# Layer-norm boundaries whose GpSimd work goes to VectorE, and eight more weight tiles split early and kept in DRAM

## The chip, the cores and the metric

The kernel runs on one core of one Trainium2 chip. The metric is device microseconds (us) of one execution. TensorE is called PE, VectorE DVE, ScalarE ACT, GpSimd POOL, and SyncE, which issues nearly every transfer, SP.

## The reference, cut to what matters

Two layers over 512 frames of width 1024. Layer 0 mixes with gated linear attention (GLA), layer 1 with chunked softmax attention (16 heads); each is followed by a squared-ReLU MLP of width 4096. Four times, after each mixer and each MLP, comes a layer norm:

```python
u = x * (1.0 + sc1) + sh1
y = gla_mixer(u, ...) if layer == 0 else chunk_attention(u, ...)
x = layer_norm(ALPHA * x + (1.0 + g1) * y, ln_g[i, 0], ln_b[i, 0])
u = x * (1.0 + sc2) + sh2
y = squared_relu_mlp(u, ff_w1[i], ff_w2[i])
x = layer_norm(ALPHA * x + (1.0 + g2) * y, ln_g[i, 1], ln_b[i, 1])
```

Shift, scale and gate come from a conditioning vector through `w_ada`. Everything is float32, and the result has to keep close to float32 precision.

## The kernel before, in words

**Layout.** Features lie on the 128 partitions, so x is eight tiles `xs[0..7]` of 128x512 (features x frames). A layer norm is a sum over partitions and over the eight tiles.

**Split weights.** Each weight is cut into 512 KB tiles of 128x1024. A tile is loaded (`raw`), cast to a short format on ACT (`whi`), and the rest is formed on DVE (`wlo = raw - whi`). Each product is three matmuls (`mm3`: hi·hi, hi·lo, lo·hi). The order of this work is the list `plan`; `fill(n)` walks it until n tiles are ready. Kinds of unit: `w` and `p` load and split into the four `wp` slots (`p` with the subtraction on POOL), `f` and `F` into tiles of the `act` pool (first products of the next MLP), `a` is a unit of `w_ada`, `c` loads and splits a tile and writes both halves to DRAM, and `x`, `X` read such halves back. There are five `raw` slots. In before, 18 tiles are kept in this way: 14 of `a_qk` (attention's q and k projections) and four of `a_o` (its output projection).

**Order.** Instructions on DVE, ACT, POOL and PE are issued in the order in which the program calls them (`InOrder`); each engine executes its own list in order. SP's list is put in order by the scheduler.

**A boundary.** `boundary()` finishes the output products of a mixer or MLP, adds them to x, and normalises. Tiles 0 to 3 are finished first (`part`, `ev`), then tiles 4 to 7 in two halves of 256 frames (`half_mm`, `half_ev`). To keep the variance exact, a common shift is subtracted from x first (`shift_mm`). Two accumulators hold the sum (`accz`) and the sum of squares (`accq`); in the names of the trace both are `af`, as are the squares. `stats1(hf)` sums them over partitions with `ones_c` on PE, forms the variance (`ve`) and 1/sqrt; `stats2` refines it (`y`). Then every tile is centred (minus the mean `ps`, or its copy `mn`), scaled by `y`, and turned into the next u (`ar`: hi on ACT, lo on DVE). The first four products of the next MLP (`fg`) take u half by half, 96 matmuls of 256 columns for each half. In before, POOL does a part of the subtractions of the shift, most of the sums of squares, the centring and scaling of the odd tiles and five small products (`ln_cols`).

Four boundaries are run: B1 after GLA (about 200 to 261 us), B2 after MLP 0 (about 560 to 608), B3 after attention (about 805 to 876; with `late` order), B4 after MLP 1 (the last 20 us; its output is the result). B2 has no `fg`: its u goes to the value passes of attention (`vfill`: `v_mm(0,fw,0)`, `v_mm(1,vw,0)`, `v_mm(0,fw,1)`, `v_mm(1,vw,1)`), which use `a_v` kept in `act` tiles (`fhi`, `flo`) and `wp` tiles. Behind the value passes come the products of q and k, first with `a_qk[0]`, then `a_qk[8]`. Their weights are, in before, the next two `w` units of the plan; the 14 others are read back from DRAM.

Of the kernel before, what the change touches and what calls it, by code (L numbers as in the profile page):

```python
# [59 lines left out]
def trunk(ctx, tc, xT, c, ada, cols, gk1, gk2, w_qk, w_v, w_g, w_go, a_qk, a_v, a_tab,  # L60
# [128 lines left out]
    def emit_unit():  # L189
# [26 lines left out]
        lo_of(G if kind in "pF" else V, lo, raw, hi)  # L216
# [70 lines left out]
    add_units([a_v[k] for k in range(4, 8)])  # L287
    add_units([a_qk[0], a_qk[8]])
# [18 lines left out]
    def ln_cols(l, i, nxt):  # L307
# [4 lines left out]
        if nxt is not None:  # L312
# [5 lines left out]
            tt(G, a1, g, mS, ALU.mult)  # L318
            tt(G, b1, b, mS, ALU.mult)
            tt(G, b1, b1, mH, ALU.add)  # L320
            ag = const.tile([P, 8], F32, name=nm("ag"))
            ab = const.tile([P, 8], F32, name=nm("ab"))
            G.tensor_scalar(out=ag, in0=g, scalar1=ALPHA, scalar2=None, op0=ALU.mult)
            G.tensor_scalar(out=ab, in0=b, scalar1=ALPHA, scalar2=None, op0=ALU.mult)
# [5 lines left out]
    def boundary(src, l, gt, open_lnt, mk_cols, fg_evac, events=None, final=False, vfill=None):  # L330
# [25 lines left out]
        def ev(m):  # L356
            stt(xs[m], pss[m], mod(l, gt, m), xs[m], ALU.mult, ALU.add)
            if m == 1:
                tt(V, accz, xs[0], xs[1], ALU.add)

        def shift_mm():
            pm = bank()
            T.matmul(pm, ones_h, accz, start=True, stop=True)
            A.copy(out=shift, in_=pm)
            for j in (4, 5, 6, 7):
                if j > 5 or "shift" in events:
                    tt(G, xs[j], xs[j], shift, ALU.subtract)
                else:
                    tt(V, xs[j], xs[j], shift, ALU.subtract)
            for j in (0, 1):  # L370
                tt(V, xs[j], xs[j], shift, ALU.subtract)

        events = events or [(0, range(8)), (1, range(8)), (2, range(8)), "shift", (3, range(8))]
        late = "shift" not in events
        for e in events:
            if e == "shift":
                shift_mm()
                continue
# [5 lines left out]
            if left[m] == 0:  # L384
                ev(m)
                if m < 3 and "shift" in events:
                    fill(3)
        lnc = mk_cols()
# [3 lines left out]
        def start_acc():  # L392
            for m in (2, 3):
                tt(V, xs[m], xs[m], shift, ALU.subtract)
            tt(V, accz, xs[0], xs[1], ALU.add)
            A.activation(out=accq, in_=xs[0], func=AF.Square)
            tt(G if "shift" in events else V, accq, accq, sq_of(xs[1], S), ALU.add)
            for m in (2, 3):
                tt(V, accz, accz, xs[m], ALU.add)
                if late and m == 3:  # L400
                    q = shift
                    A.activation(out=q, in_=xs[m], func=AF.Square)
                else:
                    q = sq_of(xs[m], S)
                tt(G, accq, accq, q, ALU.add)

        if "shift" in events:
            start_acc()
        else:
            fill_f(4)  # L410
# [6 lines left out]
        def half_ev(m, hf, ps, j, mid=lambda: None):  # L417
            hs = slice(hf * HT, (hf + 1) * HT)
            xh = xs[m][:, hs]
            stt(xh, ps[:, j * HT:(j + 1) * HT], mod(l, gt, m), xh, ALU.mult, ALU.add)  # L420
# [5 lines left out]
            tt(V if m == 7 or (final and hf) else G, accq[:, hs], accq[:, hs], q, ALU.add)  # L426
# [6 lines left out]
        def stats1(hf, last=None, fill_in=None):  # L433
# [24 lines left out]
            for k in (2, 4):  # L458
                tt(V, xs[k][:, hs], xs[k][:, hs], dm, ALU.subtract)
            st[hf] = dm, ve, y0  # L460

        def stats2(hf):
            hs = slice(hf * HT, (hf + 1) * HT)
# [3 lines left out]
            tt(V, xs[6][:, hs], xs[6][:, hs], dm, ALU.subtract)  # L467
# [3 lines left out]
            st[hf] = y  # L471
            for k in (1, 3, 7) if final and hf else (1, 3, 5, 7):
                tt(G, xs[k][:, hs], xs[k][:, hs], y, ALU.mult)
# [4 lines left out]
        def ap1(hf, p):  # L478
            ks = (2 * p, 2 * p + 1)
            hs = slice(hf * HT, (hf + 1) * HT)  # L480
            k = ks[0]
            tt(V, xs[k][:, hs], xs[k][:, hs], st[hf], ALU.mult)
            for k in ks:
                xh = xs[k][:, hs]
                a1, b1 = lnc["a"][:, k:k + 1], lnc["b1"][:, k:k + 1]
                us[k] = tl("u", 4)
                A.activation(out=un[k][:, 0, hs], in_=xh, func=AF.Identity, scale=a1, bias=b1)
                if k % 2:
                    V.tensor_scalar(out=us[k], in0=xh, scalar1=a1, scalar2=b1, op0=ALU.mult, op1=ALU.add)
                else:  # L490
                    A.activation(out=us[k], in_=xh, func=AF.Identity, scale=a1, bias=b1)

        def ap2(hf, p):
            hs = slice(hf * HT, (hf + 1) * HT)
            for k in (2 * p, 2 * p + 1):
                lo_of(V, un[k][:, 1, hs], us[k], un[k][:, 0, hs])

        def norm(hf, k):
            hs = slice(hf * HT, (hf + 1) * HT)
            tt(V, xs[k][:, hs], xs[k][:, hs], st[hf], ALU.mult)  # L500
# [20 lines left out]
        for m in range(4, 8):  # L521
            pa[m] = bank()
            half_mm(m, 0, pa[m], 0)
            if m == 4 and "shift" not in events:
                shift_mm()
                start_acc()
            half_ev(m, 0, pa[m], 0)
        pb = {m: bank() for m in range(4, 8)}
        half_mm(4, 1, pb[4], 0)
        if late:  # L530
            half_mm(5, 1, pb[5], 0, range(3))
            half_ev(4, 1, pb[4], 0)
            stats1(0)
            half_mm(5, 1, pb[5], 0, range(3, KT))
            stats2(0)
        else:
            stats1(0)
            stats2(0)
            half_ev(4, 1, pb[4], 0, (lambda: norm(0, 0)) if final else lambda: None)
            half_mm(5, 1, pb[5], 0)  # L540
        if final:
            affine(0, 1, (1, 3))
            affine(0, 0, (0, 2))
            half_ev(5, 1, pb[5], 0, lambda: norm(0, 2))
            half_mm(6, 1, pb[6], 0)
            affine(0, 3, (1, 3))
            affine(0, 2, (0, 2))
            half_ev(6, 1, pb[6], 0)
            half_mm(7, 1, pb[7], 0)
            affine(0, 5, (5, 7))  # L550

# [4 lines left out]
            stats1(1, lambda: half_ev(7, 1, pb[7], 0), fill_in)  # L556
            affine(0, 7, (5, 7))
            affine(0, 4, (4, 6))
            affine(0, 6, (4, 6))
            stats2(1)  # L560
            norm(1, 0)
            affine(1, 0, (0,))
            norm(1, 2)
            affine(1, 2, (2,))
            affine(1, 1, (1,), True)
            norm(1, 4)
            affine(1, 4, (4, 5))
            norm(1, 5)
            affine(1, 5, (4, 5))
            norm(1, 6)  # L570
            affine(1, 3, (3, 6), True)
            affine(1, 6, (3, 6), True)
            affine(1, 7, (7,))
            return None
        ap1(0, 0)
        half_ev(5, 1, pb[5], 0)
        ap1(0, 1)
        ap2(0, 0)
        half_mm(6, 1, pb[6], 0)
        half_ev(6, 1, pb[6], 0)  # L580
        ap1(0, 2)
        ap2(0, 1)
        half_mm(7, 1, pb[7], 0)
        half_ev(7, 1, pb[7], 0)
# [9 lines left out]
        n = 3 if late else 2  # L594
# [703 lines left out]
```

## Time and profile before

| what | value |
|---|---|
| median of 3 runs | 1222.27 us (1222.24 to 1222.6) |
| the profiled execution | 1222.72 us |
| its span, first to last instruction | 1220.9 us |
| mean granted TensorE clock | 0.990 |
| busy: PE, DVE, ACT, POOL | 1181.6, 831.1, 544.8, 176.6 us |
| HBM read, written | 174.37 MB, 20.97 MB |

Busy time of PE comes close to the span, and so the idle stretches of PE, and those at half clock, are what can be won or lost. All times within the program are counted from the start of the span.

### The profile page before, as it was taken

The page shows a single profiled execution, that of the slowest core. Times are in us where ns is not written, and L with a number is a line of the kernel's source. Part 1 is how long each engine was busy: PE and PEld are TensorE (multiplying, and loading weights), DVE is VectorE, ACT ScalarE, POOL GpSimd, SP SyncE. Part 2 cuts the span into 40 slices and gives each one's busy share as a digit, 9 for nine tenths or more (in the row PEclk, how much of TensorE's full clock was granted, in tenths as well). Part 3 has the DMA queues.
Part 4 walks back from the last instruction along what each step waited for, and adds up shares of the span by engine and source line. Part 5 has one row for each costly group of instructions (what it writes and reads, how often), then busy time and mean ns, then how long its engine had stood idle before and what let it go on. Part 6 is the DMA issues. An engine that isn't in the chain of part 4 may idle for free.

```text
span 1220.9 us, 15202 instructions
## 1 busy us (share of the span) xinstructions
PE 1181.6 (97%) x5742; PEld 985.9 (81%) x5742; DVE 831.1 (68%) x1260; ACT 544.8 (45%) x853; POOL 176.6 (14%) x189
## 2 busy tenths in 40 slices
PE   9999999899999999999899999998999999999995
PEld 5888888788888888888788786678888888888885
DVE  6788589777676677658834878898764443443467
ACT  4564545474243342342536656654641422322324
POOL 1000003610000000005511222235200000000035
PEclk9999999999999999999999999999899999999998
DMA  9756435028889889844026431321155232332201
GB/s 350 257 187 218 170 104 188 3 76 306 291 302 344 295 301 336 297 157 156 31 74 224 155 118 63 130 85 55 62 196 152 90 104 86 102 105 88 94 10 69
DMA packets 58282, 196.33 MB, mean 161 GB/s; under 512 B 6561, under 2 KB 10913, under 8 KB 58210
## 3 DMA queue, kind: packets, MB, share of 16 engines
q1 hardware_dynamic: 58210, 195.37, 46.1%
q8 instruction: 45, 0.74, 0.2%
q14 instruction: 27, 0.22, 0.1%
HBM read 174.37 MB, written 20.97 MB: 160 GB/s over the span
## 4 chain that ended last, share of the span: by engine, by line
PE 77%; DVE 13%; ACT 4%; POOL 3%; issue 2%; ACTq 0%; DVEq 0%; POOLq 0%
PE ps L47 76%; DVE af L47 5%; DVE x L47 3%; ACT af L47 2%; DVE ar L47 2%; POOL af L47 1%; DVE u L47 1%; POOL x L47 1%; DVE wlo L47 1%; PE warm L47 1%; ACT ar L47 1%; DVE d L47 1%; DVE y L47 1%; DVE t L47 0%; DVE raw L47 0%
## 5 line engine op out<-in xcount | busy, mean ns | idle before, releaser
L47 PE MATMUL ps<-ar,whi 128*128 128x512 f32 (+1 forms) x2880 | 822.1, 373 | 0.2 <-DVE ar L47 0.2
L47 PEld LDWEIGHTS ps<-ar,whi 128*128 128x128 f32 x2880 | 526.7, 190 | 96.4 <-issue 2.4
L47 PE MATMUL ps<-ar,wlo 128*128 128x512 f32 (+1 forms) x1440 | 526.0, 372 | 0.2 <-DVE wlo L47 0.2
L47 PEld LDWEIGHTS ps<-ar,wlo 128*128 128x128 f32 x1440 | 273.3, 190 | 46.9 <-DVE wlo L47 0.8
L47 ACT CAST whi<-raw 128x1024 fp32r<-128x1024 f32 (+1 forms) x169 | 169.5, 1010 | 204.8 <-PE ps L47 168.6
L47 DVE TENSOR_TENSOR wlo<-raw,whi 128x1024 fp32r<-128x1024 f32 x160 | 200.2, 1256 | 20.9 <-ACT whi L47 19.1
L47 DVE SCALAR_TENSOR_TENSOR x<-ps,mods,x 128x512 f32<-128x512 f32 (+1 forms) x96 | 63.0, 657 | 123.1 <-PE ps L47 123.1
L47 POOL TENSOR_TENSOR x<-x,af 128x512 f32<-128x512 f32 x14 | 25.4, 1843 | 808.7 <-ACT af L47 808.7
L47 DVE TENSOR_TENSOR h<-r 128x512 f32<-128x512 f32 (+1 forms) x72 | 49.2, 688 | 85.5 <-ACT r L47 84.7
L47 ACT ACTIVATE r<-ps 128x512 f32<-128x512 f32 (+1 forms) x72 | 39.1, 549 | 133.0 <-PE ps L47 132.8
L47 DVE SCALAR_TENSOR_TENSOR raw<-raw,csil 128x1024 f32<-128x1024 f32 x80 | 96.8, 1217 | 0.0
L47 PE MATMUL ps<-ar,fhi 128*128 128x256 f32 (+1 forms) x320 | 70.9, 317 | 6.8 <-DVE ar L47 5.9
L47 DVE TENSOR_TENSOR ar<-h,ar 128x512 fp32r<-128x512 f32 (+1 forms) x72 | 45.6, 633 | 39.5 <-ACT ar L47 38.4
L47 ACT CAST ar<-h 128x512 fp32r<-128x512 f32 (+1 forms) x72 | 41.2, 572 | 51.0 <-DVE h L47 51.0
L47 PEld LDWEIGHTS ps<-ar,fhi 128*128 128x128 f32 x320 | 53.9, 198 | 10.6 <-DVE ar L47 7.1
L47 PE MATMUL ps<-whi,ar 128*128 128x512 f32 x192 | 60.6, 390 | 0.0
L47 POOL PARTITION_ALL_REDUCE mb<-af x16 | 31.7, 1984 | 131.0 <-DVE af L47 123.9
L47 PE MATMUL ps<-ar,flo 128*128 128x256 f32 (+1 forms) x160 | 49.9, 312 | 0.0
L47 ACT ACTIVATE af<-x 128x256 f32<-128x256 f32 (+1 forms) x48 | 22.7, 486 | 57.6 <-POOL af L47 31.8
L47 PEld LDWEIGHTS ps<-whi,ar 128*128 128x128 f32 x192 | 36.0, 188 | 7.6
L47 ACT CAST fhi<-raw 128x1024 fp32r<-128x1024 f32 x30 | 31.4, 1049 | 23.7 <-DMA raw<-a_qk 12.2
L47 ACT ACTIVATE af<-af 128x1024 f32<-128x1024 f32 (+2 forms) x48 | 32.0, 698 | 20.9 <-DVE af L47 20.4
(149 smaller groups left out, 1139.4 us busy)
## 6 DMA issues: line engine op xcount, KB each, us to landing
raw<-f SPq DMA_DIRECT2D x128, 512.0 KB, 4.3
raw<-ada SPq DMA_DIRECT2D x80, 512.0 KB, 4.6
hraw<-ada SPq DMA_DIRECT2D x16, 512.0 KB, 9.0
raw<-a_qk SPq DMA_DIRECT2D x16, 512.0 KB, 5.4
khi_q<-fhi SPq DMA_DIRECT2D x14, 512.0 KB, 3.6
klo_q<-flo SPq DMA_DIRECT2D x14, 512.0 KB, 4.9
whi<-khi_q SPq DMA_DIRECT2D x14, 512.0 KB, 3.3
wlo<-klo_q SPq DMA_DIRECT2D x14, 512.0 KB, 4.3
```

What stands on the lines that cost most here:

```text
L47: r = f(*a, **k)
```

## The change

Three things are done.

First, in all four boundaries POOL's work goes to DVE: subtraction of the shift, sums of squares, centring, scaling, the five small products, and the subtraction of `p` and `F` units. The copy `mn` of the mean goes; u of the odd tiles goes from DVE to ACT. The order within a boundary is written anew with smaller helpers (`sub`, `cen`, `ap`, `lo`). Second, the shift is taken from tile 0 alone (times 2) in place of the sum of tiles 0 and 1. Third, eight more `c` units (`a_o` 4 to 7 and the first four tiles of MLP 1, `f1[1]` 0 to 3) stand in the plan behind the last `a_v` tiles and ahead of `a_qk[0]` and `a_qk[8]`; at the end of attention these eight tiles are read back (`x`, and the new kind `Y`, which reads into `act` tiles) instead of being loaded and split there.

```diff
@@ emit_unit
-        if kind in "xX":
-            hi, lo = split_w(kind == "X")
+        if kind in "xXY":
+            hi, lo = split_w(kind != "x")
...
-            ready_w.append((hi, lo))
+            (ready_f if kind == "Y" else ready_w).append((hi, lo))
...
-        lo_of(G if kind in "pF" else V, lo, raw, hi)
+        lo_of(V, lo, raw, hi)
@@ add_out
-            plan.append(("X", ("o", i)) if early and i < 4 else ("p" if i < pool else "w", u))
+            plan.append(("X" if i < 4 else "x", ("o", i)) if early else ("w", u))
...
-            plan.extend(("fF"[i // 2], u) for i, u in enumerate(fgs))
+            plan.extend(("Y", ("f", i)) for i in range(4))
@@ the plan
     add_units([a_v[k] for k in range(4, 8)])
+    more = [(("o", i), a_o[i]) for i in range(4, 8)] + [(("f", i), f1[1, i]) for i in range(4)]
+    for m in more:
+        plan.append(("c", m))
     add_units([a_qk[0], a_qk[8]])
@@ boundary
+        def sub(*js):
+            for j in js:
+                tt(V, xs[j], xs[j], shift, ALU.subtract)
 
         def shift_mm():
             pm = bank()
-            T.matmul(pm, ones_h, accz, start=True, stop=True)
-            A.copy(out=shift, in_=pm)
-            for j in (4, 5, 6, 7):
-                if j > 5 or "shift" in events:
-                    tt(G, xs[j], xs[j], shift, ALU.subtract)
...
+            T.matmul(pm, ones_h, xs[0], start=True, stop=True)
+            A.activation(out=shift, in_=pm, func=AF.Copy, scale=2.0)
...
             if e == "shift":
                 shift_mm()
+                if not late:
+                    sub(4, 5, 6, 7, 0, 1, 2)
...
         def start_acc():
-            for m in (2, 3):
-                tt(V, xs[m], xs[m], shift, ALU.subtract)
-            tt(V, accz, xs[0], xs[1], ALU.add)
             A.activation(out=accq, in_=xs[0], func=AF.Square)
-            tt(G if "shift" in events else V, accq, accq, sq_of(xs[1], S), ALU.add)
...
+            q = [shs[:, 1, :], shs[:, 1 if late else 0, :]]
+            for m in (1, 2, 3):
+                A.activation(out=q[m % 2], in_=xs[m], func=AF.Square)
+                tt(V, accz, xs[0] if m == 1 else accz, xs[m], ALU.add)
+                tt(V, accq, accq, q[m % 2], ALU.add)
...
             mid()
-            tt(V if m == 7 or (final and hf) else G, accq[:, hs], accq[:, hs], q, ALU.add)
+            tt(V, accq[:, hs], accq[:, hs], q, ALU.add)
...
-            mn = tl("mn", 1)
-            A.copy(out=mn, in_=dm)
...
-            for k in (1, 3, 5, 7):
-                tt(G, xs[k][:, hs], xs[k][:, hs], mn, ALU.subtract)
...
+            cen(hf, *range(n0))
...
-            for k in (1, 3, 7) if final and hf else (1, 3, 5, 7):
-                tt(G, xs[k][:, hs], xs[k][:, hs], y, ALU.mult)
...
+        half_ev(4, 1, pb[4], lambda: stats1(0, 2))
+        stats2(0)
+        half_mm(5, 1, pb[5], 0)
+        ap(0, 0, 1)
+        lo(0, 0)
+        half_ev(5, 1, pb[5])
+        cen(0, 2, 3)
```

**How it moves instructions: SP, ahead of the first q product.** In before, SP's list goes from the last `a_v` load straight to the two loads of `a_qk`, which are followed by loads for later and by the first read-back of a kept tile (`khi_q`, `klo_q` are the halves in DRAM):

```order
L213 DMA raw_5196<-a_v 128x1024
L213 DMA raw_5385<-a_qk 128x1024
L213 DMA raw_5391<-a_qk 128x1024
L213 DMA raw_6749<-a_o 128x1024
L213 DMA raw_6793<-a_o 128x1024
L213 DMA raw_6799<-a_o 128x1024
L980 DMA tab_c<-a_tab 128x16
L213 DMA raw_6805<-a_o 128x1024
L213 DMA raw_6886<-f 128x1024
L197 DMA whi_5457<-khi_q_2536 128x1024
```

Of the change, the same place. Five loads of `c` units and eight writes stand above these rows; the rows begin with the writes of the fifth unit, and the load of `a_qk[0]` is the last:

```order
L209 DMA khi_f_5421<-fhi_5417 128x1024
L210 DMA klo_f_5422<-flo_5418 128x1024
L204 DMA raw_5425<-f 128x1024
L204 DMA raw_5435<-f 128x1024
L204 DMA raw_5445<-f 128x1024
L209 DMA khi_f_5431<-fhi_5427 128x1024
L210 DMA klo_f_5432<-flo_5428 128x1024
L209 DMA khi_f_5441<-fhi_5437 128x1024
L210 DMA klo_f_5442<-flo_5438 128x1024
L209 DMA khi_f_5451<-fhi_5447 128x1024
L210 DMA klo_f_5452<-flo_5448 128x1024
L213 DMA raw_5455<-a_qk 128x1024
```

The loads of `a_qk` have moved behind eight loads and sixteen writes of the `c` units. On ACT the eight casts, and on DVE the eight subtractions, of these units stand behind the `vt` copies that follow `v_mm(0,fw,1)` and ahead of the cast and subtraction of `a_qk[0]`.

**DVE in B1, from the last half of the first 256 frames on.** Of before; `af_1561` holds both accumulators, `af_1562` the squares, `x_94` to `x_101` are `xs[0..7]`:

```order
L47 TENSOR_TENSOR af_1561<-af_1561,x_101 128x256
L47 TENSOR_TENSOR af_1561<-af_1561,af_1562 128x256
L47 SCALAR_TENSOR_TENSOR ve_1923<-ps_1916,d_1919 128x256
L47 TENSOR_TENSOR x_94<-x_94,ps_1916 128x256
L47 TENSOR_TENSOR x_96<-x_96,ps_1916 128x256
L47 TENSOR_TENSOR x_98<-x_98,ps_1916 128x256
L47 TENSOR_TENSOR d_1936<-y_1932 128x256
L47 TENSOR_TENSOR x_100<-x_100,ps_1916 128x256
L47 SCALAR_TENSOR_TENSOR d_1936<-d_1936,ve_1923 128x256
L47 SCALAR_TENSOR_TENSOR y_1940<-d_1936,y_1932 128x256
L47 SCALAR_TENSOR_TENSOR x_98<-ps_1888,mods,x_98 128x256
L47 TENSOR_TENSOR af_1561<-af_1561,x_98 128x256
```

Of the change:

```order
L47 TENSOR_TENSOR af_1570<-af_1570,x_101 128x256
L47 TENSOR_TENSOR af_1570<-af_1570,af_1571 128x256
L47 SCALAR_TENSOR_TENSOR x_98<-ps_1887,mods,x_98 128x256
L47 TENSOR_TENSOR af_1570<-af_1570,x_98 128x256
L47 SCALAR_TENSOR_TENSOR ve_1923<-ps_1918,d_1921 128x256
L47 TENSOR_TENSOR x_94<-x_94,ps_1918 128x256
L47 TENSOR_TENSOR x_95<-x_95,ps_1918 128x256
L47 TENSOR_TENSOR af_1570<-af_1570,af_1571 128x256
L47 TENSOR_TENSOR d_1932<-y_1927 128x256
L47 SCALAR_TENSOR_TENSOR d_1932<-d_1932,ve_1923 128x256
L47 SCALAR_TENSOR_TENSOR y_1935<-d_1932,y_1927 128x256
L47 TENSOR_TENSOR x_94<-x_94,y_1935 128x256
```

The next tile's addition (`x_98<-ps`) has moved up into the wait for the statistics, only two tiles are centred ahead of `y`, and the odd tile `x_95` is now DVE's. From `ve` to the eighth lo part of u for the first 256 frames DVE has 44 instructions in this new order. POOL's list shrinks from 166 rows to 58, and none of these is left in a boundary.

## Rows read from the trace of the kernel before

**Rows 1.** Waits, whole span: us in total, times, longest us

```profile
PE ps L47 <- DVE af L47: 12.6, 9, 3.8
```

**Rows 2.** Timeline of PE, B1: start, us, what, count [idle before <- releaser]

```profile
223.24 1.22 PE L47 MATMUL ps<-af,ones_c 128*128 128x256 f32 x2 [3.81 <-DVE af L47]
...
249.78 0.39 PE L47 MATMUL ps<-ar,fhi 128*128 128x256 f32 x1 [1.56 <-DVE ar L47]
...
261.27 0.63 PE L47 MATMUL ps<-ar,whi 128*128 128x512 f32 x2
```

**Rows 3.** Timeline of DVE, B1

```profile
201.71 2.40 DVE L47 TENSOR_TENSOR x<-x,af 128x512 f32<-128x512 f32 x2 [0.75 <-ACT af L47]
...
210.75 1.29 DVE L47 TENSOR_TENSOR x<-x,af 128x512 f32<-128x512 f32 x2
...
222.76 0.42 DVE L47 TENSOR_TENSOR af<-af,af 128x256 f32<-128x256 f32 x1 [4.08 <-POOL af L47]
```

**Rows 4.** Timeline of POOL, B1

```profile
201.83 7.92 POOL L47 TENSOR_TENSOR x<-x,af 128x512 f32<-128x512 f32 x4 [195.00 <-ACT af L47]
```

**Rows 5.** Timeline of DVE, B3 and the end of attention

```profile
809.18 3.50 DVE L47 TENSOR_TENSOR wlo<-raw,whi 128x1024 fp32r<-128x1024 f32 x3
...
849.23 0.47 DVE L47 SCALAR_TENSOR_TENSOR x<-ps,mods,x 128x256 f32<-128x256 f32 x1
...
850.66 0.42 DVE L47 TENSOR_TENSOR x<-x,y 128x256 f32<-128x256 f32 x1
851.00 0.40 DVE L47 TENSOR_SCALAR u<-x,a,b 128x256 f32<-128x256 f32 x1
```

**Rows 6.** Timeline of PE, end of attention and B3

```profile
813.40 0.50 PE L47 MATMUL ps<-ar,fhi 128*128 128x512 f32 x1 [1.60 <-DVE ar L47]
...
835.51 0.70 PE L47 MATMUL ps<-af,ones_c 128*128 128x256 f32 x2 [2.99 <-DVE af L47]
836.55 0.70 PE L47 MATMUL ps<-af,ones_c 128*128 128x256 f32 x2 [0.34 <-DVE af L47]
...
861.78 0.58 PE L47 MATMUL ps<-ar,fhi 128*128 128x256 f32 x1 [2.34 <-DVE ar L47]
...
875.96 0.63 PE L47 MATMUL ps<-ar,whi 128*128 128x512 f32 x2
```

**Rows 7.** Stretches of 25 us: PE, PEld, DVE, ACT, POOL busy, PEclk, DMA, GB/s

```profile
625.00:650.00 25.00, 25.00 (x112) 20.72 (x111) 5.36 (x7) 8.08 (x12) 0.00 (x0) 1.00 0.45 168
...
850.00:875.00 25.00, 22.52 (x160) 22.02 (x159) 19.90 (x41) 13.91 (x30) 8.79 (x9) 0.86 0.06 23
```

**Rows 8.** Timeline of PE, last value pass and first q product

```profile
629.87 0.39 PE L47 MATMUL ps<-whi,ar 128*128 128x512 f32 x1
...
640.75 0.62 PE L47 MATMUL ps<-ar,whi 128*128 128x512 f32 x2
```

**Rows 9.** Timeline of ACT, value passes

```profile
629.39 0.59 ACT L47 COPY vt<-ps 128x512 f32<-128x512 f32 x1 [9.83 <-PE ps L47]
632.79 1.05 ACT L47 CAST whi<-raw 128x1024 fp32r<-128x1024 f32 x1 [2.81 <-PE ps L47]
```

**Rows 10.** Transfers, 605 to 607: issues, KB each, us from issue to landing

```profile
raw<-a_qk SPq DMA_DIRECT2D x1, 512.0 KB, 3.4
```

**Rows 11.** Transfers, 10 to 28, where loads alone are issued

```profile
DMA packets 2307, 7.35 MB, mean 409 GB/s; under 512 B 256, under 2 KB 256, under 8 KB 2307
```

**Rows 12.** Transfers, 471 to 474, where writes of kept tiles and loads mix

```profile
klo_o<-flo SPq DMA_DIRECT2D x1, 512.0 KB, 5.5
raw<-a_o SPq DMA_DIRECT2D x1, 512.0 KB, 6.3
```

**Rows 13.** Timeline of all engines, B4

```profile
1208.08 0.63 PE L47 MATMUL ps<-af,ones_c 128*128 128x256 f32 x2
...
1212.46 1.29 DVE L47 TENSOR_TENSOR x<-x,y 128x256 f32<-128x256 f32 x2
1212.57 2.49 POOL L47 TENSOR_TENSOR x<-x,y 128x256 f32<-128x256 f32 x3 [0.42 <-DVE y L47]
```

More of the change, by code (lines that the diff above doesn't have):

```diff
@@ L328, in trunk, with boundary @@
     cur = {}
-    def boundary(src, l, gt, open_lnt, mk_cols, fg_evac, events=None, final=False, vfill=None):
+    def boundary(src, l, gt, open_lnt, mk_cols, fg_evac, events=None, final=False, vfill=None, late=False):
+        lnc = mk_cols()
         acc = act_f()
@@ L385, in boundary @@
                 ev(m)
-                if m < 3 and "shift" in events:
+                if m < 3 and not late:
                     fill(3)
-        lnc = mk_cols()
         lnt = open_lnt()
@@ L392, in start_acc @@
         def start_acc():
-            for m in (2, 3):
-                tt(V, xs[m], xs[m], shift, ALU.subtract)
-            tt(V, accz, xs[0], xs[1], ALU.add)
             A.activation(out=accq, in_=xs[0], func=AF.Square)
-            tt(G if "shift" in events else V, accq, accq, sq_of(xs[1], S), ALU.add)
[L398 to L407, printed above, removed]
+            q = [shs[:, 1, :], shs[:, 1 if late else 0, :]]
[3 more added lines that the diff above has]
+                tt(V, accq, accq, q[m % 2], ALU.add)
+        if late:
+            fill_f(4)
+        else:
+            sub(3)
             start_acc()
-        else:
-            fill_f(4)
         def half_mm(m, hf, ps, j, ks=range(KT)):
@@ L431, in tl, with cen, stats1 @@
             return lnt.tile([P, HT], F32, tag=tag, bufs=bufs, name=nm(tag))
-        def stats1(hf, last=None, fill_in=None):
+        def cen(hf, *ks):
+            hs = slice(hf * HT, (hf + 1) * HT)
+            for k in ks:
+                tt(V, xs[k][:, hs], xs[k][:, hs], st[hf][0], ALU.subtract)
+        def stats1(hf, n0, last=None, fill_in=None):
             hs = slice(hf * HT, (hf + 1) * HT)
@@ L523, in boundary @@
             half_mm(m, 0, pa[m], 0)
[L524 to L527, printed above, removed]
+            if late:
+                if m == 4:
+                    sub(4, 0, 1, 2, 3)
+                    start_acc()
+                else:
+                    sub(m)
+            half_ev(m, 0, pa[m])
         pb = {m: bank() for m in range(4, 8)}
         half_mm(4, 1, pb[4], 0)
[L530 to L534, printed above, removed]
+        if final:
+            stats1(0, 4)
             stats2(0)
[L536 to L539, printed above, removed]
+            half_ev(4, 1, pb[4], lambda: norm(0, 0))
             half_mm(5, 1, pb[5], 0)
-        if final:
+            affine(0, 0, (0, 2))
+            cen(0, 4, 5)
+            norm(0, 1)
             affine(0, 1, (1, 3))
-            affine(0, 0, (0, 2))
-            half_ev(5, 1, pb[5], 0, lambda: norm(0, 2))
+            half_ev(5, 1, pb[5], lambda: norm(0, 2))
             half_mm(6, 1, pb[6], 0)
+            affine(0, 2, (0, 2))
+            norm(0, 3)
             affine(0, 3, (1, 3))
-            affine(0, 2, (0, 2))
-            half_ev(6, 1, pb[6], 0)
+            cen(0, 6, 7)
+            half_ev(6, 1, pb[6], lambda: norm(0, 5))
             half_mm(7, 1, pb[7], 0)
             affine(0, 5, (5, 7))
+            norm(0, 7)
+            affine(0, 7, (5, 7))
             def fill_in():
@@ L593, in boundary, with second, third @@
         fa = None if vfill else [bank(), bank()]
-        n = 3 if late else 2
+        n = 3
+        def second():
+            ap(0, 5)
+            lo(0, 4)
+            stats1(1, 2)
+            cen(0, 6, 7)
+            ap(0, 6)
+            lo(0, 5)
+            stats2(1)
+            ap(0, 7)
+            lo(0, 6, 7)
+        def third():
+            ap(1, 0, 1)
+            for k in range(2, KT):
+                cen(1, k)
+                ap(1, k)
+                lo(1, k - 2)
+            lo(1, KT - 2, KT - 1)
         if vfill:
@@ L622, in boundary @@
             fg(0, fa, range(n))
-            ap1(0, 3)
-            ap2(0, 2)
-            stats1(1)
-            ap2(0, 3)
-            stats2(1)
-            fg(0, fa, range(n, 8))
-            ap1(1, 0)
-            for p in range(1, 4):
-                ap1(1, p)
-                ap2(1, p - 1)
-            ap2(1, 3)
+            second()
+            fg(0, fa, range(n, 8))
+            third()
             fb = [bank(), bank()]
@@ L1183, in att @@
               (0, (5,)), (1, (5,)), (2, (5,)), (3, range(6)), (0, (6,)), (1, (6,)), (2, (6,)), (3, (6,)),
[L1184 removed]
+              (0, (7,)), (1, (7,)), (2, (7,)), "shift", (3, (7,))]
         return o, ev, es
@@ L1241, in trunk @@
     evac_h, run = mlp_fns()
-    u = boundary(o, 1, G1, opener(es, 1), lambda: ln_cols(1, 0, (1, SH2, SC2)), evac_h, ev)
+    u = boundary(o, 1, G1, opener(es, 1), lambda: ln_cols(1, 0, (1, SH2, SC2)), evac_h, ev, late=True)
     hs = run(u, 1)
```

95 lines of the change are left out of this document (37 added, 58 removed).

## The prediction, as it was put on record

> **What bounds the kernel now.** I read the busy times first: PE is busy in nearly all of the span, so only idle PE time and PE time at half clock can be moved. The waits say who ends PE's idle time. PE waits nine times for an accumulator that DVE writes, 12.6 us in all [rows 1], and these are the layer norms. In B1 it stands 3.81 us until it may sum the squares at 223.24, and again 1.56 us before the second half of `fg` [rows 2]. DVE had itself stood 4.08 us for POOL's last sum of squares [rows 3]: the chain in B1 runs through POOL. While POOL subtracted the shift, 1.98 us a tile [rows 4], DVE's own two subtractions took 2.40 us; two of the same form with less beside them took 1.29 [rows 3]. B3 looks alike (2.99, 0.34 and 2.34 us), with 1.60 us ahead of it for the last attention output [rows 6]. Three `wlo` subtractions of 3.50 us had stood in front of that on DVE [rows 5]. The clock comes on top: from 850 to 875 PE was granted 0.86 [rows 7], that is 0.14 x 25 = 3.5 us lost.
>
> The stage into which the third part of the change puts its units is of the other kind. From 625 to 650 PE is busy all the time at full clock, while DVE works 5.4 and ACT 8.1 of 25 us [rows 7]. There PE goes from the last value pass (begun at 629.87) at 640.75 to the first q product without a gap [rows 8].
>
> **Boundaries.** Call Q the time at which PE may sum the squares of the first half.
>
> *B1, up to Q.* DVE now has seven shift subtractions at 1.29 / 2 = 0.64 at most (0.60 from start to start), from 201.7: 205.9. One addition of a finished tile (0.65) and three lo subtractions at 3.50 / 3 = 1.17 [rows 5] bring it to 210.0; one more subtraction and six accumulations of 512 columns at about 0.64 to 214.5. Four half tiles follow. An undisturbed addition of a half tile, with its sum, square and sum of squares, takes 850.66 - 849.23 = 1.43 [rows 5], so Q = 214.5 + 5.7 = 220.3 in place of 223.24: 2.9 us.
>
> *From Q on.* Variance to first scaling took 1212.46 - 1208.08 = 4.4 us in B4, with POOL beside [rows 13]; I take 4.05. Undisturbed DVE instructions of 256 columns follow each other at 851.00 - 850.66 = 0.34 [rows 5]. The 44 instructions to the eighth lo part take about 0.40 on average (some depend on the one before), 17.6 us; with 0.75 until the variance and about 3.7 of waits for ACT's conversions the last lo part is there at Q + 22. The first half of `fg` then ends at Q + 23.5, the second (96 matmuls, 261.27 - 249.78 = 11.5 us [rows 2]) at Q + 35.5 with half a microsecond lost. Before, that was 38.0. So `fg` ends at 255.8 in place of 261.27: **-5.5**. An instruction of this form takes POOL 2.49 / 3 = 0.83 us [rows 13] and DVE 0.34, which is why moving it can shorten a chain although DVE's list gets longer.
>
> *B2.* The nine waits [rows 1] less the three of 3.81, 2.99 and 0.34 us leave 5.5 us for six small ones in B1, B2 and B4, some 0.9 each. Two of them lie in B2 ahead of the value passes, and I count their end **-2.0** earlier: the last pass ends at 638.8 where it ended at 640.75.
>
> *B3.* The three subtractions in front of the last attention output are gone, since the tiles are read back: 1.60 us. If the waits of 2.99 and 0.34 us go too, Q = 836.55 - 4.9 = 831.6 (I use 831.45). `fg` ends at Q + 35.5 = 866.95 in place of 875.96: **-9.0**. The stretches at half clock are in this figure: with shorter waits ahead of them I expect none.
>
> *B4.* DVE must do seven centrings and scalings of the second half that POOL did beside it, three of them behind `y` in 2.49 us [rows 13]. They are at the end, and nothing hides them: 3 x 0.34 less what POOL's slower instructions cost, **+0.9**, with bounds 0 and +2.4 (all seven at 0.34).
>
> **The eight new `c` units.** In before, the `a_qk` load was issued between 605 and 607 and landed 3.4 us later [rows 10], long before its use; its cast at 632.79 waited only for a weight slot of PE's [rows 9]. Now it stands in SP's list behind the writes of all eight units, and those cannot start before the `vt` copy that waits for the third value pass (629.39 before [rows 9], 627.4 with B2's gain). From there, step by step:
>
> - Five units have loaded tiles. Their casts (1.05 [rows 9]) and lo subtractions (1.17) run from 627.9 to 634.9, and give ten writes of 512 KB from 629 on.
> - A transfer takes 0.524 MB / 409 GB/s = 1.28 us of the engines when they are full [rows 11]. A load between writes landed 6.3 us after issue, the write ahead of it 5.5, where a lone load takes 3.4 [rows 10, 12]: I take it that a load waits in line behind writes. The ten writes then land from 632.5 to 644.1.
> - The raw slots of the last three units are free early, but their loads stand behind those writes: issued at 635, landing at 645.4, 646.7 and 648.0. Split, they are done at 650.4.
> - Their six writes again stand ahead of `a_qk[0]`: issued at 650.8, landing 6 x 1.28 behind the first at 657.9. Cast 659.0, lo part 660.2. The third matmul of the q product needs it, so the product effectively begins at 659.8.
>
> PE, done at 638.8, stands about 21 us. Against before, 659.8 - 640.75 = **+19.1**. Behind so long an idle stretch I add **+1.5** for a low clock, by the size of the loss in [rows 7] (3.5 in all for B3's stretches), bounds 0 and 3.5. A sum with each load landing 3.4 us after its issue gives the lower bound of the stall: loads at 638.3 to 639.1, splits to 643, `a_qk[0]` issued at 643.4, landing at 646.8, split 649.1, so product at 648.6, a stall of 10 us or +7.9. The order in the lists forces this much: a load behind a write that waits for a subtraction.
>
> The reads back at the end of attention (x, Y) replace loads of half their bytes. I count them at nothing, because their slots come free as early as the loads' did, and `fg` needs the last of them only some 20 us after its issue. If one came too late, it would cost up to a lone transfer's 3.4 us [rows 10].
>
> On the line of transfers the Trainium skill (DMA: Bandwidth & Descriptors, Two DMAs through the same engine are not ordered) says that transfers of one queue start in order but are pipelined, that read and write sides of an engine are separate, and that nothing orders the 16 engines among each other. Taken alone, a load would not have to wait until the writes ahead have landed, and the sum would go by the lower bound of the stall. The trace's 6.3 us beside 3.4 speaks against that here, in a lighter mixture than the coming one.
>
> **Sum.** -5.5 (B1), +19.1 (with B2's -2.0 in it), +1.5, -9.0 (B3), +0.9 = +7.0. On the profiled execution's 1222.7 that is 1229.7; the median of the runs lies 0.45 below that execution, so **1229**.
>
> **The rivals.**
>
> *Loads don't wait in line.* The stall is 10 us; the sum is -5.5 + 7.9 + 0.5 - 9.0 + 0.9 = -5, so 1217: faster. For it: the loads read what the writes don't touch, and reading and writing may overlap; against it, the 6.3 us. It turns to faster where the stall is under 12 us.
>
> *DVE becomes the bound of the boundaries.* It takes all of POOL's 100-odd instructions, and was busy 19.9 of 25 us in B3 already [rows 7]. Were each boundary's gain from Q on lost (B1 2.5, B3 4) and the clock as low as before, the result is 1229 + 2.5 + 4 + 2 = about 1237. Against it: a large part of its busy time was the slowing beside POOL.
>
> *The units are hidden.* By its busy time DVE could take eight splits of 1.17 us between 625 and 650, and `a_qk[0]` might be loaded ahead. Then all gains stay: 1222.3 - 5.5 - 2.0 - 9.0 + 0.9 = 1207. Against it stands SP's list, where `a_qk[0]` is behind the writes. It would take another order at run time than the one listed.
>
> **How the numbers follow.** Forecast as summed 0.62; loads free of the line 0.17; DVE the bound 0.14; hidden 0.05; the rest, both signs, 0.02. The forecast's own range, from clock (0 to 3.5), tail and boundaries, is 1224 to 1235. Taking in the two rivals next to it, the range is 1217 to 1237. I take 0.2% (2.4 us) as what a measurement tells from no change. Faster than that: the first rival and the hidden case less their upper parts, 0.18. Within: the edges of the forecast and of the first rival, 0.10. Slower: 0.72.
>
> **What would show it.** In the profile of the changed kernel: PE idle some 20 us ahead of the first q product, ended by ACT's cast or DVE's `wlo`, and these in turn by a transfer `raw<-a_qk` issued only after the `f1` writes. In the boundaries: no POOL, DVE's 512-column subtractions at 0.6 us, first sum of squares at about 220 and 3.4 us less idle time there; `fg` over at 256 in B1. The idle time before the last attention output gone. The prediction is wrong if the `a_qk` load lands before 648 (the stall is then 10), if PE still waits over 3 us for the sums of squares, or if the reads back come late and PE stands at the end of attention.

## The result, and the profile after

The changed kernel takes 1228.72 us (median of 4 runs, 1227.78 to 1229.28), the kernel before 1222.26 in the same session (1222.07 to 1222.60): ratio 1.0052, 95% interval 1.0034 to 1.0069, slower by 6.5 us. The forecast was 1229. The profiled execution is the shortest of the four, 1227.78 us with a span of 1226.1 (before 1222.72 and 1220.9), so the profile has 5.2 us of span to account for.

The timeline of PE in the changed kernel, at the places that answer to [rows 2], [rows 6] and [rows 8]:

```profile
219.83 1.21 PE L47 MATMUL ps<-af,ones_c 128*128 128x256 f32 x4 [1.30 <-DVE af L47]
...
238.62 0.39 PE L47 MATMUL ps<-ar,fhi 128*128 128x256 f32 x1 [0.79 <-DVE ar L47]
...
255.22 0.63 PE L47 MATMUL ps<-ar,whi 128*128 128x512 f32 x2
...
652.99 1.22 PE L47 MATMUL ps<-ar,whi 128*128 128x512 f32 x2 [21.26 <-ACT whi L47]
...
845.30 1.21 PE L47 MATMUL ps<-af,ones_c 128*128 128x256 f32 x4 [0.75 <-DVE af L47]
...
864.04 0.39 PE L47 MATMUL ps<-ar,fhi 128*128 128x256 f32 x1 [0.73 <-DVE ar L47]
...
880.64 0.63 PE L47 MATMUL ps<-ar,whi 128*128 128x512 f32 x2
```

The boundaries are shorter, as in the first three rows: the wait of 3.81 us in B1 is 1.30, and `fg` is over at 255.22 instead of 261.27. At 652.99 stands the loss: PE waits 21.26 us for the cast of `a_qk[0]`, where before it went on without a gap. The two rows at 845.30 and 864.04 have in their brackets what 2.99, 0.34 and 2.34 us were. The waits of the changed kernel, in total, say the same (us in total, times, longest):

```profile
PE ps L47 <- ACT whi L47: 21.3, 1, 21.3
...
PE ps L47 <- DVE af L47: 2.8, 3, 1.3
```

The second row was 12.6 us in nine waits [rows 1]. How the 21 us come about is read on ACT and on SP. ACT's timeline in the changed kernel:

```profile
620.21 0.59 ACT L47 COPY vt<-ps 128x512 f32<-128x512 f32 x1 [8.99 <-PE ps L47]
620.69 4.84 ACT L47 CAST fhi<-raw 128x1024 fp32r<-128x1024 f32 x5
638.59 1.04 ACT L47 CAST fhi<-raw 128x1024 fp32r<-128x1024 f32 x1 [13.05 <-DMA raw<-f]
...
651.89 1.05 ACT L47 CAST whi<-raw 128x1024 fp32r<-128x1024 f32 x1 [9.71 <-DMA raw<-a_qk]
```

The casts of the first five units run without a wait, directly behind a `vt` copy. Then ACT stands 13.05 us for the load of the sixth unit, and 9.71 us for `a_qk[0]`. SP's timeline has the reason (the second number is how long SP took to issue):

```profile
621.77 0.33 SPq L209 DMA_DIRECT2D khi_o<-fhi  x1
...
632.29 3.01 SPq L204 DMA_DIRECT2D raw<-f  x3
...
643.96 1.17 SPq L210 DMA_DIRECT2D klo_f<-flo  x1
645.18 2.45 SPq L213 DMA_DIRECT2D raw<-a_qk  x2
```

Ten writes go out between 621.77 and 632.29. Only then are three loads issued, and behind the last six writes, at 645.18, `a_qk[0]`. It lands 6.6 us later (from the transfers of 645 to 646.4: KB each, us to landing):

```profile
raw<-a_qk SPq DMA_DIRECT2D x1, 512.0 KB, 6.6
```

One thing stays open: ACT stood idle for 8.99 us ahead of that `vt` copy, while the loads of the first five units had all been issued by 602.40. No run puts their casts ahead of the copy, so it is not known whether they could stand there and how much of the stall this place in ACT's list costs.

The clock comes last. Stretches of the changed kernel (length, then PE, PEld, DVE, ACT, POOL busy, PEclk, DMA share, GB/s):

```profile
632.00:636.00 4.00, 0.00 (x0) 0.00 (x0) 0.00 (x0) 0.00 (x0) 0.00 (x0) 1.00 1.03 352
637.00:656.00 19.00, 2.97 (x6) 1.96 (x7) 6.64 (x6) 7.01 (x8) 0.00 (x0) 0.50 0.99 385
657.00:661.00 4.00, 4.00 (x19) 3.33 (x18) 0.00 (x0) 0.20 (x1) 0.00 (x0) 1.00 0.57 227
...
850.00:875.00 25.00, 24.00 (x193) 23.28 (x193) 21.03 (x58) 18.05 (x38) 0.00 (x0) 1.00 0.00 1
```

From 637 to 656 PE stood most of the time and was granted 0.50, the lower of its two levels (1.2 of 2.4 GHz), and this reached 3 to 4 us into the work after 652.99. In the last stretch, which was at 0.86 before [rows 7], the clock is full.

### The profile page after: what moved, and what is told of

It is laid out like the page before. It is cut to its first block, busy times and chain, and to the rows that moved or that the text cites. A ratio compares the mean times of both kernels' runs of the same rounds, so it can differ in the third digit from the quotient of the medians.

```text
span 1226.1 us, 15171 instructions
## 1 busy us (share of the span) xinstructions
PE 1177.4 (96%) x5742; PEld 980.0 (80%) x5742; DVE 827.8 (68%) x1359; ACT 555.1 (45%) x870; POOL 48.9 (4%) x61
## 4 chain that ended last, share of the span: by engine, by line
PE 75%; DVE 14%; ACT 6%; issue 2%; DMA 1%; SPq 1%; DVEq 0%; ACTq 0%
PE ps L47 74%; DVE af L47 5%; DVE x L47 4%; ACT af L47 3%; ACT ar L47 1%; DVE ar L47 1%; DVE wlo L47 1%; ACT u L47 1%; PE warm L47 1%; DVE flo L47 1%; DMA raw<-a_qk 1%; DVE d L47 1%; DMA raw<-f 1%; DVE t L47 0%; DVE y L47 0%
## 5 line engine op out<-in xcount | busy, mean ns | idle before, releaser
L47 PE MATMUL ps<-ar,whi 128*128 128x512 f32 (+1 forms) x2880 | 819.1, 372 | 21.5 <-ACT whi L47 21.3
L47 ACT CAST whi<-raw 128x1024 fp32r<-128x1024 f32 (+1 forms) x165 | 165.6, 1011 | 206.1 <-PE ps L47 152.3
L47 DVE TENSOR_TENSOR wlo<-raw,whi 128x1024 fp32r<-128x1024 f32 x158 | 192.5, 1223 | 29.0 <-ACT whi L47 27.1
L47 DVE TENSOR_TENSOR h<-r 128x512 f32<-128x512 f32 (+1 forms) x72 | 45.2, 633 | 79.0 <-ACT r L47 78.1
L47 ACT CAST fhi<-raw 128x1024 fp32r<-128x1024 f32 x34 | 35.3, 1049 | 36.3 <-DMA raw<-f 15.8
L47 DVE TENSOR_TENSOR flo<-raw,fhi 128x1024 fp32r<-128x1024 f32 x34 | 41.2, 1221 | 12.8 <-ACT fhi L47 12.7
L47 ACT ACTIVATE ar<-x,b,a 128x256 fp32r<-128x256 f32 x48 | 28.6, 595 | 25.7 <-DVE x L47 25.7
```

The source lines that it names most:

```text
L47: r = f(*a, **k)
```

## The experiments

Ratios are to the kernel before, timed beside each kernel on the same chip, with 95% intervals; the changed kernel is at 1.0052.

**The boundaries alone.** Edit to the changed kernel:

```diff
-    for m in more:
-        plan.append(("c", m))
...
-            plan.append(("X" if i < 4 else "x", ("o", i)) if early else ("w", u))
+            plan.append(("X", ("o", i)) if early and i < 4 else ("w", u))
...
-            plan.extend(("Y", ("f", i)) for i in range(4))
+            plan.extend(("f", u) for u in fgs)
```

> The change's boundaries alone: the eight new c units are taken out of the plan, a_o 4 to 7 and the four f1 tiles are loaded and split at the end of attention as before (all subtractions on VectorE). Theory (the boundaries gain about 6 us in B1, 3 in B2, 7 to 8 in B3, the whole loss is the c units' stall ahead of the first q product): no long idle stretch at 630 to 650, no half clock there, and 1222.3 - 6 - 3 - 7.5 + 0.5 = about 1206. The wait of 1.6 us ahead of the last attention output stays. Rival (B3's gain came from the tiles being read back, not from the boundary): B3 from the last half tile to the end of fg keeps its old length of 43 us, and the time is about 1213.

Measured: 1211.76 us, ratio 0.9921 (0.9906 to 0.9936). No stall at 630 to 650, as the theory says, but B3 keeps a wait. The timelines of DVE and of PE in this kernel:

```profile
809.89 4.63 DVE L47 TENSOR_TENSOR flo<-raw,fhi 128x1024 fp32r<-128x1024 f32 x4 [0.17 <-ACT fhi L47]
```

```profile
828.84 1.65 PE L47 MATMUL ps<-af,ones_c 128*128 128x256 f32 x3 [5.52 <-DVE af L47]
```

Four subtractions of `f1`, 4.63 us, stand in DVE's list ahead of the shift, and PE waits 5.52 us for the sum of squares, more than the 2.99 of before. So in B1 and B2 the gain is the boundary's own (`fg` of B1 is over at 255.77 here and 255.22 in the changed kernel), while most of B3's needs the tiles to be read back. From a wait of attention that all these kernels have (784.65 in before, 776.52 here, 799.63 in the changed kernel) to the end of B3's `fg` the boundaries alone gain 2.1 us, the whole change 10.3. The rival was nearly right there, and the time lies between the two expectations.

**The units alone**, put into the kernel before (the third part of the change, with its reads `x` and `Y`; boundaries as before):

```diff
+    more = [(("o", i), a_o[i]) for i in range(4, 8)] + [(("f", i), f1[1, i]) for i in range(4)]
+    for m in more:
+        plan.append(("c", m))
     add_units([a_qk[0], a_qk[8]])
```

> The kernel before with the eight c units, x and Y alone; its boundaries with GpSimd stay. Theory: the stall ahead of the first q product is the same 21 us, with about 2 us of half clock behind it, and the end of attention gains 1.6 to 3: 1222.3 + 21 + 2 - 2.5 = about 1243. Rival (the stall exists only because the faster boundaries bring TensorE to the q product sooner): stall of about 12 us, time 1222.3 + 12 + 1.5 - 2.5 = about 1233.

Measured: 1241.97 us, ratio 1.0168 (1.0153 to 1.0183): the theory's 1243. PE's timeline:

```profile
662.34 1.22 PE L47 MATMUL ps<-ar,whi 128*128 128x512 f32 x2 [21.22 <-ACT whi L47]
```

The stall is as long with the slow boundaries as with the fast ones. It belongs to the units alone. Alone, the two parts give -9.6 us (1211.76 in a session where before had 1221.36) and +20.6 (1241.97, same session), 11.0 in sum, and together +6.5. Most of the missing 4.5 us lies in B3: over the same stretch as above the units alone gain 4.9 us and the boundaries alone 2.1, but both together 10.3. Each part frees what the other needs. Where the last microsecond goes is not shown.

**The writes on another queue.** Edit to the changed kernel (`"C"` marks the eight new units):

```diff
+            wq = nc.gpsimd if kind == "C" else nc.sync
-            nc.sync.dma_start(out=kept[key][0], in_=hi.bitcast(F32))
-            nc.sync.dma_start(out=kept[key][1], in_=lo.bitcast(F32))
+            wq.dma_start(out=kept[key][0], in_=hi.bitcast(F32))
+            wq.dma_start(out=kept[key][1], in_=lo.bitcast(F32))
```

> The changed kernel with the writes of the eight new c units issued by GpSimd's queue instead of SP's, nothing else. Theory (the load of a_qk[0] is late because it stands in SP's list behind writes that wait for subtractions): the loads no longer stand behind them, a_qk[0] is issued before 630, TensorE stands under 4 us ahead of the first q product, 1205 to 1210. Rival (the transfers' bytes are the cause: 24 transfers of 512 KB at 1.28 us are 31 us of all engines from 621 on): the a_qk[0] load shares the engines with the writes, lands after 638, the stall is 8 to 12 us and the time 1214 to 1219.

Measured: 1227.29 us, ratio 1.0048 (1.0033 to 1.0063). Both expectations missed, the theory's by far. The load of `a_qk[0]` was now issued at 627.20, when seven of the sixteen writes had been issued, but the transfers of 622 to 650 read (KB each, us to landing):

```profile
khi_f<-fhi POOLq DMA_DIRECT2D x4, 512.0 KB, 19.5
...
raw<-a_qk SPq DMA_DIRECT2D x2, 512.0 KB, 10.3
```

The two queues share the engines, and every transfer takes much longer. PE's timeline, and DVE's:

```profile
638.65 1.22 PE L47 MATMUL ps<-ar,whi 128*128 128x512 f32 x2 [6.16 <-ACT whi L47]
...
682.47 0.76 PE L47 MATMUL ps<-ar,ar 128*128 128x512 f32 x1 [11.86 <-DVE ar L47]
```

```profile
671.46 1.53 DVE L47 SCALAR_TENSOR_TENSOR af<-ps,ng,af 128x256 f32<-128x256 f32 x4 [16.95 <-DMA af<-a_win]
```

Of 21 us ahead of the first q product 6 are left, but 12 appear at 682, because DVE waited 16.95 us for a small table (`a_win`) that came behind the same bytes: up to 13.0 us to landing, where it has at most 5.1 in the changed kernel. So SP's order decides who waits. How long points to the bytes: 24 transfers of 0.524 MB take 31 us at 409 GB/s [rows 11], and they are put where PE's lead is some 10 us.

**The units behind `a_qk`.** Edit to the changed kernel:

```diff
-    for m in more:
-        plan.append(("c", m))
     add_units([a_qk[0], a_qk[8]])
+    for m in more:
+        plan.append(("c", m))
```

> The changed kernel with the eight new c units behind a_qk[0] and a_qk[8] in the plan instead of ahead of them. Theory (place, not amount, costs): a_qk[0] and a_qk[8] are loaded by 605 as before, no stall ahead of the first q product. SP's list has the writes ahead of the read back of the fourth pair's second tile, which may cost up to 5 us later in attention: 1204 to 1209. Rival (the stall only moves, since the same 24 transfers and eight splits stand in front of the next read backs): TensorE stands 10 us or more between 640 and 700, 1214 or more.

Measured: 1224.12 us, ratio 1.0020 (1.0010 to 1.0029). The rival is right, the stall moves. The timelines of ACT and of PE:

```profile
658.72 1.04 ACT L47 CAST fhi<-raw 128x1024 fp32r<-128x1024 f32 x1 [13.06 <-DMA raw<-f]
```

```profile
666.32 1.19 PE L47 MATMUL ps<-ar,ar 128*128 128x512 f32 x2 [17.95 <-DVE ar L47]
```

ACT stands the same 13 us for the sixth unit's load (13.05 in the changed kernel), now ahead of a copy of k that attention waits for. Three orders of the same 24 transfers thus cost PE 21.3, 18.0 (6.16 and 11.86) and 18.0 us.

**Four units in place of eight.** Edit to the changed kernel:

```diff
-    more = [(("o", i), a_o[i]) for i in range(4, 8)] + [(("f", i), f1[1, i]) for i in range(4)]
+    more = [(("o", i), a_o[i]) for i in range(4, 8)]
...
-            plan.extend(("Y", ("f", i)) for i in range(4))
+            plan.extend(("f", u) for u in fgs)
```

> The changed kernel with only the four a_o tiles as new c units; the four f1 tiles are loaded and split at the end of attention. Theory (the stall comes from loads that find no raw slot in time and so stand behind writes: four units leave the fifth slot to a_qk[0], which is then loaded before 605): the stall ahead of the first q product is gone, and at most 3 us appear ahead of the first k product, whose load stands behind eight writes. B3 waits some 5 us as with the boundaries alone, because four flo subtractions are back: 1211 to 1214. Rival (the stall grows with the number of units): half of 21 us, so 1220 or more.

Measured: 1210.74 us, ratio 0.9914 (0.9899 to 0.9929), just below the expected 1211 to 1214. PE's timeline:

```profile
638.52 0.50 PE L47 MATMUL ps<-ar,wlo 128*128 128x512 f32 x1 [0.53 <-DVE wlo L47]
...
827.62 1.65 PE L47 MATMUL ps<-af,ones_c 128*128 128x256 f32 x3 [5.54 <-DVE af L47]
```

Four units find raw slots ahead of time and `a_qk[0]` the fifth (its load is issued at 602.61), and of the two `a_qk` tiles only `a_qk[8]` is loaded behind writes: 0.53 us instead of 21. The `f1` subtractions cost B3 their 5.54 us as with the boundaries alone.

**The units in MLP 0, uneven and even.** Two kernels, with the eight units among the 18 old ones (both drop the loop behind the `a_v` tiles and hand the eight to the list of MLP 0); the uneven one has units behind three of five tiles:

```diff
-            if keep and i % 5 in (1, 3):
+            if keep and i % 5 in (1, 3, 4):
```

> The changed kernel with the eight new c units spread over MLP 0 among the 18 old ones (a place after 3 of 5 tiles in place of 2 of 5) instead of standing ahead of a_qk[0]. Theory: no stall ahead of the first q product, all gains stay, 1203 to 1207, and equal to or 2 us below the boundaries alone. Rival (MLP 0 has no room: its transfers run near 300 of 409 GB/s and VectorE at seven to eight tenths): TensorE gets waits for weights in MLP 0, between 280 and 500 us, of 3 to 10 us, and the time is 1208 to 1215.

and the even one behind every second tile, two of them among the first four:

```diff
+            if keep and m % 2:
+                plan.append(("c", keep.pop(0)))
...
-            if keep and i % 5 in (1, 3):
+            if keep and i % 2:
```

> The changed kernel with the eight new c units in MLP 0, placed evenly: 26 units, one behind every second weight tile, two of them already among the first four tiles, so that no two stand behind neighbouring tiles. Theory (the spread over three of five tiles lost 12 us to two bursts in which two units stood behind neighbouring tiles and 2.5 MB per 5.4 us asked more than the 409 GB/s that the transfers reach): no wait for weights over 0.5 us between 280 and 500, full clock there, no stall ahead of the first q product, 1202 to 1206. Rival (eight units more are too much for MLP 0 however they lie): waits of 3 to 8 us there again, 1210 to 1220.

Measured: uneven 1219.03 us, ratio 0.9980 (0.9971 to 0.9990), so the rival's way, with a loss above its 1208 to 1215; even 1205.45 us, ratio 0.9870 (0.9855 to 0.9884), as the theory has it. ACT, PE and a stretch of the uneven kernel:

```profile
352.50 1.05 ACT L47 CAST fhi<-raw 128x1024 fp32r<-128x1024 f32 x1 [3.80 <-DMA raw<-a_qk]
```

```profile
373.11 1.52 PE L47 MATMUL ps<-ar,whi 128*128 128x512 f32 x2 [2.80 <-ACT ar L47]
```

```profile
340.00:380.00 40.00, 36.70 (x147) 28.95 (x146) 30.27 (x41) 17.60 (x23) 0.00 (x0) 0.91 0.92 340
```

and the same stretch of the even one:

```profile
340.00:380.00 40.00, 40.00 (x178) 33.10 (x178) 30.75 (x41) 18.00 (x22) 0.00 (x0) 1.00 0.94 351
```

Both move nearly the same bytes (340 and 351 GB/s). In the uneven kernel PE waits 2.80 us at 373 for evaluated MLP products, and 3.67 us once more at 467. Half clock behind the two waits, 6.8 and 3.4 us, nearly doubles the price. With the units placed evenly PE has no such waits, so the place is shown as the cause. The way from a late load to PE is only argued: the evaluations stand behind the units' casts in ACT's list, and ACT waits 3.80 us for a unit's load at 352.50. But the even kernel has such waits on ACT too, up to 6.35 us for a load at 412.83, and PE does not stand there.

**A piece of the boundary undone**: the half tiles' sums of squares go back to POOL, in the changed kernel:

```diff
-            tt(V, accq[:, hs], accq[:, hs], q, ALU.add)
+            tt(V if m == 7 or (final and hf) else G, accq[:, hs], accq[:, hs], q, ALU.add)
```

> The changed kernel with one piece of the boundary undone: the sums of squares of the half tiles go back to GpSimd (not for tile 7, as in the kernel before). Theory (the boundary's gain is the chain through GpSimd): in B1 TensorE waits 3 us or more again for the sum of squares (1.3 us in the changed kernel), and B1 loses 2 to 3 us, B3 likewise; the stall ahead of the first q product stays 21 us, so 1232 to 1235. Rival (the gain came from the new order of the instructions, and GpSimd's part of the squares is hidden): waits as in the changed kernel and 1228 to 1230.

Measured: 1222.73 us, ratio 1.0009 (0.9999 to 1.0019), some 6 us *faster* than the changed kernel. Theory and rival both fell. The timelines of POOL, DVE and PE:

```profile
218.33 0.73 POOL L47 TENSOR_TENSOR af<-af,af 128x256 f32<-128x256 f32 x1 [0.44 <-ACT af L47]
```

```profile
218.59 0.75 DVE L47 TENSOR_TENSOR af<-af,x 128x256 f32<-128x256 f32 x1
219.26 0.41 DVE L47 TENSOR_TENSOR af<-af,af 128x256 f32<-128x256 f32 x1
```

```profile
219.40 1.13 PE L47 MATMUL ps<-af,ones_c 128*128 128x256 f32 x4 [0.55 <-DVE af L47]
```

In the boundary POOL has nothing else to do now, and takes each square as soon as ACT has formed it. Ahead of the first sum of squares two DVE instructions that run beside POOL take 0.78 and 0.75 us in place of 0.42, but three of 0.42 and their places in the list are taken from DVE. In the changed kernel DVE has no idle time from 212.40 until this sum is ready at 220.3, so there DVE itself bounds the boundary. The stall ahead of the first q product is unchanged (21.1 us); in the profiled executions the gain is 1.7 us in B1 (`fg` over at 253.87 for 255.22, with a start 0.3 later), 1.3 in B2 and 1.9 in B3, 4.6 in the span. The medians differ by 6.0, and by 5.8 against the kernel before of each session.

**One piece of the change alone**, in the kernel before: the subtraction of the shift goes from POOL to DVE, all else of the boundary stays.

```diff
-                if j > 5 or "shift" in events:
-                    tt(G, xs[j], xs[j], shift, ALU.subtract)
-                else:
-                    tt(V, xs[j], xs[j], shift, ALU.subtract)
+                tt(V, xs[j], xs[j], shift, ALU.subtract)
```

> The kernel before with one piece of the change: the subtraction of the shift from tiles 4 to 7 goes from GpSimd to VectorE, all else of the boundary stays on GpSimd. Theory (GpSimd's chain was late in B1 because four subtractions of 1.98 us stood ahead of the sums of squares): the wait of 3.8 us for the sum of squares in B1 shrinks below 1.5, that in B3 likewise, and the time is 1213 to 1218. Rival (the centring and scaling on GpSimd, and its slowing of VectorE, hold the boundary, so that the wait only moves behind the statistics): 1219 to 1223.

Measured: 1215.45 us, ratio 0.9947 (0.9931 to 0.9964): the time and B1 as the theory has them, B3 not. DVE and PE:

```profile
220.56 0.43 DVE L47 TENSOR_TENSOR af<-af,af 128x256 f32<-128x256 f32 x1 [1.42 <-POOL af L47]
```

```profile
221.04 0.89 PE L47 MATMUL ps<-af,ones_c 128*128 128x256 f32 x2 [1.15 <-DVE af L47]
...
247.27 0.39 PE L47 MATMUL ps<-ar,fhi 128*128 128x256 f32 x1 [1.56 <-DVE ar L47]
...
830.17 0.70 PE L47 MATMUL ps<-af,ones_c 128*128 128x256 f32 x2 [2.04 <-DVE af L47]
```

In B1 DVE's wait for POOL fell from 4.08 us [rows 3] to 1.42, PE's from 3.81 to 1.15. The 1.56 us ahead of the second half of `fg` stay, to the hundredth, which points to the centring and scaling that are still on POOL. In B3 PE's wait fell only from 2.99 us [rows 6] to 2.04, where below 1.5 was expected: there two of the four subtractions had been on DVE before. Of B1's gain this piece alone brings 2.5 us (`fg` over at 258.76 for 261.27); the change has 6.05, and what the new order, the shift from tile 0 alone and the centring and scaling on DVE each have of the rest was not separated.

**Both lessons together**: units spread evenly, half tiles' squares on POOL (the two edits above).

> The evenly spread units together with the half tiles' sums of squares on GpSimd. Theory now (with GpSimd free of all else, these sums lie beside VectorE's work, and VectorE, which bounds the boundaries of the change, is relieved): the gains add, 1205.5 - 5 = about 1200, no wait over 0.6 us for a sum of squares in B1, B2 and B3. Rival (the 6 us of the earlier run came through the stall ahead of the first q product, which was only reached earlier): 1203 to 1206.

Measured: 1199.76 us, ratio 0.9821 (0.9807 to 0.9836). The gains add. PE's waits in this kernel:

```profile
PE ps L47 <- DVE af L47: 1.3, 2, 0.8
```

The 0.8 us is B4's; in B1 it is 0.54, and in B2 and B3 there is none. This version beats the kernel before by 22 us, timed beside it, and the changed kernel, timed in another session, by 29.

## Why the prediction was right, step by step

**The stall.** Forecast 21 us, measured 21.26, in the changed kernel and in three others that keep the units ahead of `a_qk[0]` or in a burst (21.22, 21.1, and 17.95 where moved). Most steps held as well, with B1's gain of 5.5 taken off their times, which the prediction had entered only in the sum: casts from 622.4 (measured 620.69), the sixth unit's load landing at 639.9 (cast at 638.59), `a_qk[0]` issued at 645.3 (645.18), landing at 652.4 (cast at 651.89), the product at 654.3 (652.99). In between two errors cancelled: the three loads behind the first ten writes were issued at 632.29 and not at 629.5, because SP needed up to 1.2 us to issue a write, and they then took 6.3 us to landing and not 10.4. The disputed step, that loads wait in line behind writes, is right: 6.6 us to landing where a lone load has 3.4 [rows 10]. So the other reading, with its lower bound of a 10 us stall, is out. The Trainium skill (DMA: Bandwidth & Descriptors, Two DMAs through the same engine are not ordered) says that nothing orders transfers across the 16 engines. That doesn't make a load fast: the DMA engines were busy for 0.99 of 637 to 656, and the load took its 6.6 us. One sentence of mine said too little: that the order in the lists forces at least 10 us of the stall. The kernel with the writes on POOL's queue undid that order and lost 18 us all the same, 6 of them at this place.

**The clock.** Forecast +1.5. The distance to the kernel before is 12.24 us at the first q product (652.99 and 640.75) and 14.45 at the next wait that both have (749.25 and 734.80): +2.2. The 3 to 4 us at half clock after 652.99 explain 1.5 to 2 of it.

**B1.** Forecast 5.5, measured 6.05 (255.22 for 261.27); the sum of squares was to be ready at 220.3, and DVE ended it at 220.3:

```profile
219.86 0.42 DVE L47 TENSOR_TENSOR af<-af,af 128x256 f32<-128x256 f32 x1
```

**B2.** Forecast 2.0. PE was done with the value passes at 652.99 - 21.26 = 631.73; before, their last matmul ended at 640.91. Of these 9.2 us B1 has 6.05, which leaves 3.1. The prediction counted two waits of about 0.9. Three of 3.12 us in sum became one of 0.74, and the granted clock of 575 to 600, which the prediction left out, went from 0.93 to 1.00.

**B3.** Forecast 9.0. The distance of 14.98 us ahead of the last attention outputs is 4.68 at the end of `fg` (880.64 and 875.96): 10.3. The size was nearly right, its source only in part, so this is partly luck: I counted the waits of 2.99 and 0.34 us as the boundary's, but with the boundaries alone the wait is 5.52 and the gain 2.1. What frees B3 is that `f1` subtractions have left DVE's list as well (two in the kernel before, four with the boundaries alone), which my sum did not name.

**B4.** Forecast +0.9; the last output is issued at 1223.23 for 1217.48, 5.75 us later, where 4.68 came in: +1.1.

With +0.5 that attention lost at one wait for ACT (1.17 for 0.64 us at 799.63), and 0.6 less for the last landing, the terms give -6.05 - 3.1 + 21.4 + 2.2 + 0.5 - 10.3 + 1.1 - 0.6 = 5.2, the difference of the spans. (21.4 is the wait of 21.26 and 0.16, since before the q product began 0.16 us ahead of the end that the profile gives the last value pass.)

That the median came within 0.3 us of the 1229 is luck. For the profiled execution the sum gave 1229.7, and it took 1227.78. The rest was made good because I took the median to lie 0.45 us below the profiled execution, and it lay 0.94 above.

**What was wrong in it.** The rival "DVE becomes the bound" got 0.14 as something that would eat the gain. It is true and does not eat it: DVE bounds the new boundaries up to the sum of squares, and the squares' move is a loss of 5 to 6 us inside a gain. My sentence that 0.34 us on DVE for 0.83 on POOL shortens a chain holds for the shift's subtractions, and fails for the half tiles' squares, where POOL had the time.

## What to carry to other kernels

Work that is moved to an earlier stage brings its transfers along: count the bytes against the time until the next needed load, not the busy time of the engines that do the arithmetic (DVE had 20 of 25 us free where PE then stood 21). Place such units one by one where each has its slack, and look for neighbours. When a slow helper engine is relieved, move what is ahead of the path's end first, measure, and keep on the helper what then lies beside other work.

## What the runs showed of the hardware

Two queues gave no more bandwidth. With eight writes each of hi and lo on POOL's queue beside SP's loads, the transfers of 622 to 650 moved 366 GB/s, with one queue in the changed kernel 371. The `a_qk` loads took 10.3 us and the writes up to 19.5, for 6.6 and under 6 with one queue. Behind several writes in a row SP itself is held at the issue: 1.1 to 1.2 us for each of the writes from 624.78 to 629.76, where the first took 0.33. In the stall of 21 us, PE was granted the full clock from 632 to 636 and the lower level from 637 to 656, which reached 3 to 4 us into its work; from 657 to 661 the clock was full again.
